# A decoder layer whose front end runs in segments of two, two and four token tiles instead of one, three and four

## The chip, the cores and the metric

One core of one Trainium2 chip runs the whole program; x holds 1024 tokens of 1024 features. The metric is the device time of one execution in microseconds; the kernel before has a median of 3162.57 us over 3 runs (3149.99 to 3165.83).

## What is computed

A decoder layer with adaLN modulation: shift, scale and gate vectors come from `silu(c) @ ada_w + ada_b`. The first half mixes tokens, with 8 retention heads and 8 stick-breaking attention heads behind one input projection and in front of one output projection. The second half is PEER, a layer of 16384 single-neuron experts of which each token picks 16 per head, 8 heads. Cut to what matters:

```python
h = rms_norm(x, norm1_gain) * (1 + scale1) + shift1
r_q, r_k, r_v, r_g, s_q, s_k, s_v = split(h @ w_in)            # 7 x 512 columns
y_ret = head_group_norm(retention(r_q, r_k, r_v)) * silu(r_g)
y_sb  = rms_norm(stick_breaking(rms_norm(s_q), rms_norm(s_k), s_v))
x = x + gate1 * (concat(y_ret, y_sb) @ w_out)
h2 = rms_norm(x, norm2_gain) * (1 + scale2) + shift2
# PEER, per token and head:
top_s, top_i = top_k(sub_scores(h2 @ w_query, sub_keys), 16)   # both halves of the query
best, ids = top_k(all sums of the two halves, 16)
act = gelu(h2 . down[ids]) * softmax(best)
x = x + gate2 * sum(act * up[ids])
```

## The kernel before, in words

The 1024 tokens are 8 token tiles of 128. The program has a front end, which goes through the tiles in segments, and two ways of computing PEER.

**The front end**, `seg_gen`, handles one segment of `nt` tiles from tile `t0`; `SEGS` (L25) lists the segments, (0,1), (1,3), (4,4). For its tiles a segment does, in this order: rms norm and transposition (`to_T`); seven streams of w_in (rk, rq, rv, rg, K, Q, V), each 8 weight blocks of 128x512 floats (256 KB); retention between the streams; stick-breaking attention, in units of a tile and a pair of heads; two streams of w_out; the residual, a second norm and transposition; four streams of wq, whose scores go to a top-16 on VectorE (`top16`), and the top-k over pairs (`topk`). That is 56, 16 and 32 weight blocks in each segment, whatever its number of tiles. The adaLN passes (`mod_pass`, L141) have 16, 16 and 8 loads of 512 KB in segment 0 and a smaller one in segment 1.

**`stream`** has two paths. With one tile (`whole`), weights come two blocks in one load of 512 KB into the pool `u`, 13 buffers (L256), and are multiplied as plain float32 (L261, L263). With more tiles the products are split float32r: each block is loaded into `wraw`, three buffers (L266); ScalarE copies it to the rounded `whi` (L71); POOL subtracts to get the rest, `wlo` (L271; VectorE for the first block of a stream, kt = 0); PE makes three products per tile, hi x hi, hi x lo, lo x hi (L275 to L281). The other operand is split likewise: `put` writes `Tlo` with a VectorE subtraction (L297).

**Tiles 0 to 3** use gathered expert rows (`gather_tile`): for each of the 128 picks of a token an indirect DMA issued by POOL brings a row of `down` for every token of the tile (L774, 512 KB), and VectorE takes the dot product (L785); then 128 times a row of `up` (L774) and an accumulation on VectorE (L795). That is 256 gathers a tile, 1024 in all, through four buffers `g`. The routing of tile 0 is made in four pieces of two heads (`topk(..., 2 * g, 2)`), each after its wq stream, so that gathers can start early; tiles 1 and 2 get theirs in one call for 8 heads; tile 3's scores go to DRAM and are routed late.

**Tiles 4 to 7** are computed densely against all experts (`dense`): first products from L826, second from L932, gate matrices built from one-hots (L865). Its first gate products follow the last piece of tile 4's routing.

**What sets the order.** A scheduler orders the instructions of each engine at build time, so any change of the program text moves rows everywhere. One tie is put in by hand: `HOLD = 480`; gathers 480 to 495 are issued only after the POOL operation of dense chunk 4, so no gather beyond 480 runs while the dense half builds its first gates.

The part that the change edits, at the end of the routing:

```python
        if t0 == 0:
            return []
        late = []
        for i in own[t0 == NG:]:
            f = lambda i=i: topk(kp, tv[i], ix[i], t0 + i, 0, 8)
            if t0 < NG:
                f()
            else:
                late.append(f)
```

`own` are the segment's tiles other than tile 3; `own[True:]` leaves out the first of them, which was routed in pieces.

Of the kernel before, what the change touches and what calls it, by code (L numbers as in the profile page):

```python
# [21 lines left out]
KT = D // 128  # L22
EPS = 1e-6
NT = 8
SEGS = [(0, 1), (1, 3), (4, 4)]  # L25
NG = 4
TD = (NT - NG) * 128
GB = 4
# [26 lines left out]
def tile_kernel(ctx, tc, A, out):  # L55
# [174 lines left out]
    def seg_gen(phase, t0, nt, hooks):  # L230
# [345 lines left out]
        for u in units:  # L576
            pend.append(u + (sb_weights(*u),))
            while after and len(pend) > 1:
                i = int(after.pop(0)[1])
# [49 lines left out]
        own = [i for i, t in enumerate(tiles) if t not in sc_d]  # L629
        tv = {i: kp.tile([128, 8, 2, 16], F32, name=f"tv{i}") for i in own}  # L630
        ix = {i: kp.tile([128, 8, 2, 16], U32, name=f"ix{i}") for i in own}
        for g in range(4):
# [18 lines left out]
            stream(A["wq"], 512 * g, hT[t0], ev_q, True)  # L651
            if t0 in (0, NG):
                topk(kp, tv[0][:, 2 * g:2 * g + 2], ix[0][:, 2 * g:2 * g + 2], t0, 2 * g, 2)
        if t0 == 0:
            return []
        late = []
        for i in own[t0 == NG:]:
            f = lambda i=i: topk(kp, tv[i], ix[i], t0 + i, 0, 8)
            if t0 < NG:
                f()  # L660
            else:
                late.append(f)
# [302 lines left out]
    with tc.tile_pool(name="tp", bufs=1) as tp_:  # L965
        kpg = tc.tile_pool(name="kp", bufs=1, side="right")
        kp = kpg.__enter__()
        with tc.tile_pool(name="att", bufs=1) as att:
            kTr = att.tile([128, 4, 1024], F32, name="kTr")
            vr = att.tile([128, NT, 512], F32, name="vr")  # L970
            state = att.tile([128, 4, 128], F32, name="state")
            POOL.memset(state, 0.0)
            with tc.tile_pool(name="wp", bufs=1) as wp, tc.tile_pool(name="up", bufs=13) as up, \
                    tc.tile_pool(name="vp", bufs=9) as vp:
                late = []
                for s in SEGS:
                    late = seg_gen((wp, tp_, up, vp, kp), *s, late)
        with tc.tile_pool(name="dp", bufs=1, reuse_waits="tile") as dp:
            hold = dense(*hT[NG], dp, kpg, late)
# [57 lines left out]
```

## Time and profile before

| | before |
|---|---|
| median of 3 runs | 3162.57 us (3149.99 to 3165.83) |
| the profiled execution's own time | 3159.11 us |
| its span | 3157.3 us |
| granted TensorE clock, mean | 0.914 |
| PE busy | 2680.1 us (85%) |
| VectorE (DVE) busy | 2539.2 us (80%) |
| POOL busy | 1938.5 us (61%) |
| ScalarE (ACT) busy | 1297.0 us (41%) |
| chain that ended last | DVE 24%, DMA 23%, PE 18%, issue 17%, POOL 14% |

Busy shares are means over the whole span. The kernel has stages with different limits, so the tables by stage (busy time of each engine in a stretch, in us from the span's start) say more than the page's totals; the timeline tells when the front end passes a given step. The stages of the profiled execution: segment 0 up to about 220 us, with the first gathers from 198 us; segment 1 from there to 766 us (first rotation at 259.51); segment 2 to 1505 us; then the dense half.

### The profile page before, as it was taken

What the parts mean: (1) busy time and instruction counts of PE and PEld (TensorE: products, weight loads), DVE (VectorE), ACT (ScalarE), POOL (GpSimd) and SP (SyncE); (2) the same over time, 40 slices, a digit from 0 to 9 for tenths busy, and PEclk for the clock granted to TensorE, in tenths of its full rate; (3) what the DMA queues carried; (4) which work ended last, traced back from release to release, by engine and by line L of the source; (5) the groups of instructions that cost most, each with busy time, mean ns of one, the idle gap of its engine ahead of it and who ended that gap; (6) DMA issues with size and microseconds to landing.
All of it is one profiled execution on the core that took longest, in us unless ns stands there. A gap on an engine that the chain in (4) does not pass through costs nothing.

```text
span 3157.3 us, 38775 instructions
## 1 busy us (share of the span) xinstructions
PE 2680.1 (85%) x12308; PEld 2078.8 (66%) x12308; DVE 2539.2 (80%) x4677; ACT 1297.0 (41%) x2254; POOL 1938.5 (61%) x1590
## 2 busy tenths in 40 slices
PE   6967878697886888762878999889999999999997
PEld 2454654486664446652767887677778878878886
DVE  2269788789988997899999778997767777777788
ACT  1232334344332652421666744454444434444441
POOL 1126775677777677652568756556666567666664
PEclk9978985899987879885999999999999999999998
DMA  8788877897867778882268889889989999999998
GB/s 320 252 295 285 285 250 248 298 341 254 268 228 243 226 238 281 299 279 95 111 238 328 313 304 328 282 303 318 332 308 332 323 332 334 332 328 332 321 337 273
DMA packets 337644, 899.20 MB, mean 285 GB/s; under 512 B 38296, under 2 KB 105880, under 8 KB 333344
## 3 DMA queue, kind: packets, MB, share of 16 engines
q0 software_dynamic: 147456, 536.94, 49.0%
q1 hardware_dynamic: 189984, 359.80, 32.9%
q8 instruction: 97, 1.59, 0.2%
q14 instruction: 107, 0.88, 0.1%
HBM read 846.24 MB, written 50.35 MB: 284 GB/s over the span
## 4 chain that ended last, share of the span: by engine, by line
DVE 24%; DMA 23%; PE 18%; issue 17%; POOL 14%; ACT 3%; SPq 1%; POOLq 0%; DVEq 0%; ACTq 0%
DMA g<-in_up_dram,ids 10%; POOL g L774 9%; DVE g L785 4%; DMA g<-in_down_dram,ids 4%; DVE gy L795 4%; DMA rawu<-in_up_dram 3%; PE acc L263 2%; DMA gm<-gd 2%; POOL u L817 2%; PE tp L826 2%; PE tp L827 2%; PE tp L828 2%; DVE dlo L817 1%; DVE p L865 1%; PE acc L932 1%
## 5 line engine op out<-in xcount | busy, mean ns | idle before, releaser
L774 POOL DMA_INDIRECT g<-in_down_dram,ids x512 | 582.5, 1138 | 461.9 <-DVE g L785 283.9
L795 DVE SCALAR_TENSOR_TENSOR gy<-g,a,gy 128x1024 f32<-128x1024 f32 x508 | 651.7, 1283 | 169.8 <-DMA g<-in_up_dram,ids 165.3
L774 POOL DMA_INDIRECT g<-in_up_dram,ids x512 | 552.2, 1078 | 364.5 <-DVE gy L795 197.4
L785 DVE SCALAR_TENSOR_TENSOR g<-g,gy 128x1024 f32<-128x1024 f32 x512 | 616.2, 1213 | 147.4 <-DMA g<-in_down_dram,ids 145.0
L826 PE MATMUL tp<-Thi,dhi 128*128 128x512 f32 x1024 | 405.2, 396 | 48.6 <-ACT dhi L71 45.3
L932 PE MATMUL acc<-u,p 128*128 128x512 f32 x1024 | 399.2, 399 | 42.9 <-ACT p L71 32.0
L828 PE MATMUL tp<-Thi,dlo 128*128 128x512 f32 x1024 | 402.8, 393 | 4.5 <-POOL dlo L817 4.0
L933 PE MATMUL acc<-u,p 128*128 128x512 f32 x1024 | 403.3, 397 | 0.0
L827 PE MATMUL tp<-Tlo,dhi 128*128 128x512 f32 x1024 | 403.1, 394 | 0.0
L934 PE MATMUL acc<-u,p 128*128 128x512 f32 x1024 | 385.1, 394 | 6.2 <-DVE p L911 6.1
L817 POOL TENSOR_TENSOR u<-rawu,u 128x1024 fp32r<-128x1024 f32 x128 | 308.9, 2415 | 53.1 <-ACT u L71 49.2
L271 POOL TENSOR_TENSOR wlo<-wraw,whi 128x512 fp32r<-128x512 f32 x182 | 236.0, 1304 | 61.6 <-ACT whi L71 33.9
L932 PEld LDWEIGHTS acc<-u,p 128*128 128x128 f32 x1024 | 196.3, 192 | 93.2 <-ACT p L71 37.9
L71 ACT ACTIVATE whi<-wraw 128x512 fp32r<-128x512 f32 x208 | 130.5, 630 | 308.5 <-DMA wraw<-in_w_in_dram 96.1
L817 DVE TENSOR_TENSOR dlo<-rawd,dhi 128x1024 fp32r<-128x1024 f32 x122 | 209.2, 1715 | 57.5 <-ACT dhi L71 54.6
L826 PEld LDWEIGHTS tp<-Thi,dhi 128*128 128x128 f32 x1024 | 194.4, 190 | 91.2 <-ACT dhi L71 46.3
L280 PE MATMUL acc<-wlo,Thi 128*128 128x512 f32 x504 | 213.2, 423 | 21.9 <-POOL wlo L271 19.5
L934 PEld LDWEIGHTS acc<-u,p 128*128 128x128 f32 x1024 | 194.6, 191 | 50.0 <-DVE p L911 9.6
L828 PEld LDWEIGHTS tp<-Thi,dlo 128*128 128x128 f32 x1024 | 194.4, 190 | 46.3 <-POOL dlo L817 5.1
L933 PEld LDWEIGHTS acc<-u,p 128*128 128x128 f32 x1024 | 196.5, 192 | 40.7
L827 PEld LDWEIGHTS tp<-Tlo,dhi 128*128 128x128 f32 x1024 | 194.6, 190 | 39.5
L71 ACT ACTIVATE u<-rawu 128x1024 fp32r<-128x1024 f32 x128 | 135.1, 1057 | 189.4 <-DMA rawu<-in_up_dram 182.1
(271 smaller groups left out, 5058.7 us busy)
## 6 DMA issues: line engine op xcount, KB each, us to landing
rawd<-in_downT_dram SPq DMA_DIRECT2D x128, 512.0 KB
rawu<-in_up_dram SPq DMA_DIRECT2D x128, 512.0 KB
gd<-u SPq DMA_DIRECT2D x32, 1024.0 KB
gm<-gd SPq DMA_DIRECT2D x512, 64.0 KB
wraw<-in_w_in_dram SPq DMA_DIRECT2D x112, 256.0 KB
u<-in_ada_w_dram SPq DMA_DIRECT2D x46, 512.0 KB
wraw<-in_wq_dram SPq DMA_DIRECT2D x64, 256.0 KB
u<-in_w_in_dram SPq DMA_DIRECT2D x28, 512.0 KB
```

What stands on the lines that cost most here:

```text
L71: ACT.activation(out_, in_, AF.Copy, scale=scale)
L271: (POOL if kt else DVE).tensor_sub(lo, raw, hi.bitcast(F32))
L774: POOL.indirect_dma_start(out=g, out_offset=None, in_=A[src], in_offset=bass.IndirectOffsetOnAxis(ap=groups[j // m][0][:, j % m:j % m + 1] ...
L785: DVE.scalar_tensor_tensor(g, g, 1.0, hp, op0=OP.mult, op1=OP.mult, accum_out=a[:, j:j + 1])
L795: DVE.scalar_tensor_tensor(y, g, a[:, j:j + 1], y, op0=OP.mult, op1=OP.add)
L817: eng.tensor_sub(lo, raw, hi.bitcast(F32))
L826: PE.matmul(a, dhi[:, sl], Hhi[:, kt], start=kt == 0, stop=False)
L827: PE.matmul(a, dhi[:, sl], Hlo[:, kt], start=False, stop=False)
L828: PE.matmul(a, dlo[:, sl], Hhi[:, kt], start=False, stop=kt == KT - 1)
L932: PE.matmul(y, phi[:, sl], uhi[:, ds_], start=st and b == 0, stop=False, skip_group_check=True)
L933: PE.matmul(y, phi[:, sl], ulo[:, ds_], start=False, stop=False, skip_group_check=True)
L934: PE.matmul(y, plo[:, sl], uhi[:, ds_], start=False, stop=sp and b == GB - 1, skip_group_check=True)
```

## The change

```diff
-SEGS = [(0, 1), (1, 3), (4, 4)]
+SEGS = [(0, 2), (2, 2), (4, 4)]
...
             if t0 in (0, NG):
                 topk(kp, tv[0][:, 2 * g:2 * g + 2], ix[0][:, 2 * g:2 * g + 2], t0, 2 * g, 2)
-        if t0 == 0:
-            return []
         late = []
-        for i in own[t0 == NG:]:
+        for i in own[t0 in (0, NG):]:
             f = lambda i=i: topk(kp, tv[i], ix[i], t0 + i, 0, 8)
```

Segment 0 now handles tiles 0 and 1, segment 1 tiles 2 and 3. No segment has one tile, so the `whole` path of `stream`, `operand`, `put` and `to_T` is not taken any more: segment 0 loads 104 weight blocks into `wraw` and splits each, and it splits its operands. Tile 0 is still routed in pieces; tile 1's 8-head routing follows in segment 0 instead of segment 1. Lines of the changed kernel from 656 on are two lower than those named here.

The order moves on every engine. Three places follow; rows that repeat are merged with a count.

SP's queue in segment 0, before, from the last w_in weights on (`ada` is the adaLN matrix, `L256` the large weight loads):

```order
L256 DMA u<-in_w_in_dram 128x2x512 x12
L482 DMA v<-in_decay_dram 128x512 x2
L483 DMA v<-in_xi_dram 128x512
L256 DMA u<-in_w_in_dram 128x2x512 x12
L138 DMA u<-in_ada_w_dram 128x1024 x15
L146 DMA v<-in_ada_b_dram 32x512 x4
```

The same place in the changed kernel:

```order
L266 DMA wraw<-in_w_in_dram 128x512 x33
L482 DMA v<-in_decay_dram 128x512 x2
L483 DMA v<-in_xi_dram 128x512
L266 DMA wraw<-in_w_in_dram 128x512 x20
L266 DMA wraw<-in_w_out_dram 128x512 x3
L138 DMA u<-in_ada_w_dram 128x1024 x12
L146 DMA v<-in_ada_b_dram 32x512 x2
L138 DMA u<-in_ada_w_dram 128x1024 x3
```

The 15 adaLN loads of the pass for gate1 and shift2 stand behind the w_in weights in both; but those weights now go through three buffers, each of which waits for the block before it, and three blocks of w_out stand between.

PE's order around that pass in the changed kernel (L141 are its products, L151 its transposes, L515 and L517 attention scores, L535 and L543 the transposes and values of attention):

```order
L515 MATMUL acc<-kTr,u 128x128
L517 MATMUL acc<-negm,ident 128x128
L141 MATMUL acc<-u,sc_159 32x512 x20
L151 MATMUL tp<-ident,v 128x128 x4
L535 MATMUL tp<-ident,u 128x128 x2
L543 MATMUL acc<-v,vr 64x128
```

Here the first attention transposes stand behind the pass's last products, as they do in the kernel before, with `x16` in place of `x20`.

POOL's queue at the first gathers, before (L80 and L81 are a norm's power of -1/2):

```order
L80 TENSOR_SCALAR s_918<-s_918 128x1
L81 TENSOR_TENSOR s_918<-s_918,mhalf 128x1
L774 DMA g<-in_down_dram,ids_0_1106 128x1024 x15
L80 TENSOR_SCALAR s_1580<-s_1580 128x1
L81 TENSOR_TENSOR s_1580<-s_1580,mhalf 128x1
```

And in the changed kernel (L772 is the gather's line there):

```order
L271 TENSOR_TENSOR wlo<-wraw,whi 128x512 x11
L80 TENSOR_SCALAR s_1989<-s_1989 128x1
L81 TENSOR_TENSOR s_1989<-s_1989,mhalf 128x1
L80 TENSOR_SCALAR s_1996<-s_1996 128x1
L81 TENSOR_TENSOR s_1996<-s_1996,mhalf 128x1
L271 TENSOR_TENSOR wlo<-wraw,whi 128x512 x17
L772 DMA g<-in_down_dram,ids_0_2355 128x1024 x4
L271 TENSOR_TENSOR wlo<-wraw,whi 128x512 x2
L772 DMA g<-in_down_dram,ids_0_2355 128x1024 x2
```

Two weight subtractions stand ahead of the first gather in the whole of POOL's queue before, 82 now, and behind it gathers and subtractions of wq alternate.

On VectorE the gathered rows that stand ahead of a step, before and after: first rotation of segment 1: 27 and 25; first rotation of segment 2: 220 and 185; end of segment 2's wq: 456 and 419; first one-hot of the dense half: 480 and 480. The 8-head top-k of tiles 1 and 2 ends behind 225 and 248 rows before, 48 and 184 now. VectorE has 39 weight subtractions for 26 and 64 `Tlo` subtractions for 46. At the end of the program the dense half's last output products stand behind 1018 to 1022 gathered rows before, and behind 1022 to 1024 now.

## Rows read from the trace of the kernel before

**Rows 1.** The page, part 1: busy time of each engine.
```profile
PE 2680.1 (85%) x12308; PEld 2078.8 (66%) x12308; DVE 2539.2 (80%) x4677; ACT 1297.0 (41%) x2254; POOL 1938.5 (61%) x1590
```

**Rows 2.** Table by stretch: length, busy PE, PEld, DVE, ACT, POOL, clock, DMA, GB/s.
```profile
0.00:199.00 199.00, 151.87 (x623) 74.31 (x624) 56.61 (x182) 42.69 (x93) 17.73 (x34) 0.93 0.82 293
...
257.00:766.00 509.00, 404.88 (x1807) 298.73 (x1808) 435.35 (x920) 185.74 (x337) 347.96 (x323) 0.84 0.83 282
257.00:1505.00 1248.00, 943.94 (x4358) 694.46 (x4359) 1099.45 (x2470) 452.26 (x809) 819.49 (x716) 0.84 0.76 256
1800.00:3157.00 1357.00, 1294.98 (x5600) 1059.74 (x5599) 1056.03 (x1456) 577.15 (x856) 851.08 (x630) 0.98 0.91 320
```

**Rows 3.** The same table for POOL's gather issues alone (L774; in brackets their number).
```profile
199.00:257.00 58.00, 27.17 (x28) 0.80 0.85 275
257.00:766.00 509.00, 198.66 (x191) 0.84 0.83 282
766.00:1505.00 739.00, 312.18 (x261) 0.83 0.72 238
```

**Rows 4.** Groups of VectorE instructions, 257 to 766 us: busy us, mean ns, idle before.
```profile
L785 DVE SCALAR_TENSOR_TENSOR g<-g,gy 128x1024 f32<-128x1024 f32 x103 | 124.1, 1212 | 28.3 <-DMA g<-in_down_dram,ids 28.0
L795 DVE SCALAR_TENSOR_TENSOR gy<-g,a,gy 128x1024 f32<-128x1024 f32 x88 | 112.8, 1282 | 18.9 <-DMA g<-in_up_dram,ids 18.3
...
L271 DVE TENSOR_TENSOR wlo<-wraw,whi 128x512 fp32r<-128x512 f32 x13 | 14.5, 1114 | 5.8 <-ACT whi L71 4.0 <-issue 1.5
...
L670 DVE MAX8 tv<-v 128x8 f32<-128x128 f32 x32 | 7.8, 281 | 1.2 <-ACT v L71 1.2
```

**Rows 5.** Waits (us, times, longest): VectorE's, 257 to 1505; SP's queue, 230 to 800.
```profile
DVE g L785 <- DMA g<-in_down_dram,ids: 56.3, 50, 4.5
...
SPq L266 <- POOL wlo L271: 329.3, 93, 34.8
```

**Rows 6.** Timeline (start, length) of segment 0 on PE, then markers on VectorE.
```profile
38.71 1.92 PE L263 MATMUL acc<-u,Thi 128*128 128x512 f32 x2
...
105.88 5.32 PE L263 MATMUL acc<-u,Thi 128*128 128x512 f32 x12
...
125.58 0.27 PE L535 MATMUL tp<-ident,u 128*128 128x128 f32 x1
...
136.58 5.38 PE L263 MATMUL acc<-u,Thi 128*128 128x512 f32 x8
...
145.03 8.85 PE L263 MATMUL acc<-u,Thi 128*128 128x512 f32 x20
...
202.72 1.22 DVE L785 SCALAR_TENSOR_TENSOR g<-g,gy 128x1024 f32<-128x1024 f32 x1 [1.41 <-DMA g<-in_down_dram,ids]
...
259.51 0.41 DVE L347 TENSOR_TENSOR v<-acc,cosT 128x256 f32<-128x256 f32 x1
...
1504.82 2.76 DVE L865 TENSOR_TENSOR p<-iota,rb 128x1024 bf16<-128x1024 bf16 x3
```

**Rows 7.** Timeline: loads issued by SP's queue, and one block's copy on ScalarE.
```profile
88.83 25.77 SPq L138 DMA_DIRECT2D u<-in_ada_w_dram  x15
...
243.79 9.53 SPq L266 DMA_DIRECT2D wraw<-in_w_in_dram  x5
...
433.43 0.33 SPq L266 DMA_DIRECT2D wraw<-in_w_in_dram  x1
...
436.26 0.63 ACT L71 ACTIVATE whi<-wraw 128x512 fp32r<-128x512 f32 x1 [2.32 <-DMA wraw<-in_w_in_dram]
```

**Rows 8.** Timeline, 243 to 248 us: a VectorE subtraction alone and beside POOL's.
```profile
243.85 0.55 DVE L297 TENSOR_TENSOR Tlo<-v,Thi 128x384 fp32r<-128x384 f32 x1
...
245.24 2.56 POOL L271 TENSOR_TENSOR wlo<-wraw,whi 128x512 fp32r<-128x512 f32 x2
245.46 2.76 DVE L297 TENSOR_TENSOR Tlo<-v,Thi 128x384 fp32r<-128x384 f32 x1
```

## Prediction

> **What bounds the kernel now.** The page first: TensorE (PE) is busy 85% of the span, VectorE (DVE) 80% [rows 1]. Those are averages over stages with different limits, so the table by stage comes next [rows 2]. From 1800 us to the end PE is busy 1295 of 1357 us: the dense half is bound by TensorE, and the change does not touch it. From 257 to 1505 us (segments 1 and 2 of the front end) the fullest engine is VectorE, 1099.45 of 1248 us or 88%; PE has 76%, POOL 66%. Before 199 us VectorE is busy 57 us of 199: the first segment leaves it idle, since no expert row can be gathered before a token tile is routed. The gathers fill the rest: 28, 191 and 261 are issued in the next three stretches [rows 3], 480 by 1505 us, where the hold stops them and the dense half's own work begins. A gathered row costs VectorE 1.21 us (dot product) or 1.28 us (accumulation) [rows 4].
>
> So the time until about 1505 us is the start of the gathers plus VectorE's remaining work at 88%. Of the idle 12% much is waiting for gathered rows (56 us for the "down" rows alone, rows 5), which will not vanish. The change puts more front-end work into the idle first segment, but makes that segment longer: it is weighed by these two terms.
>
> **Term 1: the first segment grows.** I follow segment 0 on PE [rows 6] and replace each piece.
>
> - *Seven w_in streams, 56 blocks of 128x512.* Now they run from 38.71 to 111.2 us, 72.5 us or 1.3 us per block, with plain float32 products and large loads far ahead into 13 buffers. After, each block goes through one of three raw buffers: load, ScalarE copy, POOL subtraction. One lightly loaded pass was 2.83 us from the issue to the copy's start (433.43 to 436.26), 0.63 us of copy [rows 7] and 1.28 us of subtraction (two in 2.56 us, rows 8), with hand-overs 4.95 us; over three buffers that is 1.65 us per block. Below, today's 1.3 us bounds it; above, the 2.3 us at which five loads were issued from 243.79 us on, (9.53 - 0.33)/4 [rows 7], with gathers between POOL's subtractions. Segment 0 has no gathers during its w_in streams, so I take 1.65, the light passes: 92.5 us, **+20** (0 to +56).
> - *A second tile's retention and attention, and the adaLN pass.* One tile's attention runs on PE from 125.58 to about 136.6 us, 11 us, with its first units hidden before. The second tile has twice the keys: 11 to 20, I take 16, and 3 for its retention between streams. The adaLN pass for gate1 and shift2 has 15 loads of 512 KB that today are issued from 88.83 us on, in 25.77 us [rows 7], 22 us ahead of the streams' end; in the new SP queue they stand behind the last V weight and three blocks of w_out, some 5 us ahead of the end at best. PE's order keeps the attention's transposes behind that pass, so 14 us (111.2 to 125.58) become 21 to 26: +8. Sum **+27** (+17 to +37).
> - *w_out, 16 blocks.* Today 17.3 us (136.58 to 153.88), loaded ahead. After, 16 x 1.65 = 26.4: **+9** (+4 to +20).
> - *Norms, transposes, routing.* One more tile to normalise and transpose here, one less in segment 1; wq's 32 blocks take 53 us by the same period, not far from now: **+4** (0 to +8).
>
> Together the first rotation of segment 1, now at 259.51 us, comes **+60** later (+35 to +105, as the ends do not all meet). The order has about as many gathers before it (25 for 27). The first gather itself, now consumed at 202.72 [rows 6], slips a few us more: in POOL's queue some 82 subtractions now stand ahead of it, 22 of them of wq.
>
> POOL's subtractions also bring something into this segment that it did not have: the same Tlo subtraction takes 0.55 us alone and 2.76 us beside two POOL subtractions [rows 8]. Between wq and the first index list some 15 to 20 two-input VectorE operations are on the path; their price is 0 to 20 us. I take 0: the chain mostly waits for wq's scores anyway, and most of its operations read one tensor. The Trainium skill, "SBUF — State Buffer", on the shared port pair, says that VectorE and GpSimd hold that pair exclusively for a whole instruction and the loser blocks; the 2.76 against 0.55 agrees, and it speaks against this change. By it I would add the 20 us here.
>
> **Term 2: VectorE has less to do afterwards.** From 257 to 766 us it was busy 435.35 us [rows 2]. Gathers were 124.1 + 112.8 = 237 of it, the kt = 0 weight subtractions 14.5 (they go by blocks, not tiles) [rows 4]. That leaves 184 for three tiles, of which two have their top-16 there (5 operations x 16 x 0.281 us = 22.5 us each, rows 4) and their top-k (no one row; 0 to 30 us each, I take 12). Front end of one tile: (184 - 45 - 24)/3 = 38 us. Tile 1's 38 us and its 22.5 of top-16 move into idle time of segment 0: 61 us. Its top-k stays behind that point (48 gathers stand before it in the order). With two gathers more still to do (+2.5): 1099.45 - 61 + 2.5 = 1041 us, which at 88.1% take 1182 us instead of 1248: **-66** (-45 to -80).
>
> **Term 3: the tail.** The dense half begins behind the same 480 gathers and keeps its order, so it shifts as a block; the last gathers come some four further ahead of the last output products: **-4** (0 to -5).
>
> At nothing I cost the 13 more weight subtractions and 18 more Tlo subtractions on VectorE: they fall into its idle time in segment 0, and without it would cost 13 x 1.1 + 18 x 0.55 = 24 us. ScalarE's 104 more copies are inside the block's period above.
>
> **Sum:** +60 - 66 - 4 = -10. On the profiled execution, 3159.1 us, that is 3149; on the median of the runs, 3162.6 (the profiled one is 3.5 below it), 3152.5. I say **3150**.
>
> **Rivals.**
>
> A, *VectorE alone counts* (faster). If blocks come at 1.4 us or so and the adaLN loads hide, segment 0 grows by 40; if the moved work is the upper 74 us, term 2 is -80. 40 - 80 - 4 = -44: 3118. For: VectorE is the fullest engine, 88%. Against: SP waited 329 us for POOL's subtractions between 230 and 800 us [rows 5], so the block chain is not free.
>
> B, *the block chain sets every segment's pace* (slower). Three raw buffers give a block 2.0 us or more whatever the number of tiles. Segment 0 then grows by 60 + 88 blocks in series x 0.35 = 90, while the streams of segment 1, with one tile less, do not get shorter; what shrinks there is attention and top-16, -60 at most. 90 - 60 - 4 = +26: 3188. It decides from some 1.8 us per block, where my sum is 88 x 0.15 = 13 us worse and back at zero. For: those 329 us. Against: the light passes of 4.95 us, and no gathers between the subtractions of segment 0.
>
> C, *the port* (no change). Each two-input VectorE operation between wq and the index list waits out one POOL subtraction of 1.28 us, 15 to 20 of them: +20, so +10 in all: 3170. For: rows 8. Against: few of these operations meet a subtraction while POOL also waits for blocks.
>
> **How the numbers follow.** A measurement of this kernel can tell about 0.5%, 16 us, from no change. Forecast 0.42 (its own range 3125 to 3172: faster by over 0.5% in 0.38 of it, within in 0.55, slower in 0.07), A 0.24 (faster), C 0.10 (0.8 of it within, the rest slower), B 0.24 (0.12 of it within, else slower). Faster 0.16 + 0.24 = 0.40; within 0.23 + 0.08 + 0.03 = 0.34; slower 0.26. The range reaches A's 3118 and B's 3188 with a little beyond each: 3112 to 3192.
>
> **What would show it.** Right: segment 0's w_in streams take about 92 us; the first gather is consumed near 270 us, the first rotation of segment 1 comes near 320, the dense half's first one-hot (L865, now at 1504.82, rows 6) near 1498, with VectorE at 85 to 91% between the last two. For A the streams take 80 us and that one-hot comes before 1465; for B they take over 110 us and the one-hot comes after 1520; for C the index list comes over 20 us after its last wq score. The forecast is wrong if VectorE's share leaves 85 to 91%, or if the time from the one-hot to the end moves by over 10 us.

## The result, and the profile after

The changed kernel takes 3269.38 us (median of 4 runs, 3260.02 to 3271.95) against 3160.41 us before: ratio 1.0337, 95% interval 1.0308 to 1.0367. It is 109 us slower; forecast were 3150 us, and the range ended at 3192. The profiled execution has a span of 3268.8 us, 111.5 more than before.

The page, part 1, of the changed kernel:

```profile
PE 2708.2 (83%) x12508; PEld 2109.9 (65%) x12508; DVE 2581.4 (79%) x4708; ACT 1359.3 (42%) x2373; POOL 2053.7 (63%) x1681
```

VectorE's share hardly moved, as averages do [rows 1]; POOL has 115 us more. The markers on the timeline, with start and length (lines from 656 on are two lower here, so L783 is the gather's dot product and L863 the one-hot):

```profile
45.29 0.78 PE L279 MATMUL acc<-whi,Thi 128*128 128x512 f32 x1
...
179.41 0.27 PE L535 MATMUL tp<-ident,u 128*128 128x128 f32 x1
...
231.64 0.75 DVE L562 SCALAR_TENSOR_TENSOR v<-v,cols,tp 128x512 f32<-128x512 f32 x1 [16.86 <-PE tp L561]
...
323.94 0.16 DVE L736 SCALAR_TENSOR_TENSOR ids<-ii 128x32 int32<-128x32 f32 x1
...
328.90 1.22 DVE L783 SCALAR_TENSOR_TENSOR g<-g,gy 128x1024 f32<-128x1024 f32 x1
...
392.93 0.40 DVE L347 TENSOR_TENSOR v<-acc,cosT 128x256 f32<-128x256 f32 x1
...
1603.39 2.74 DVE L863 TENSOR_TENSOR p<-iota,rb 128x1024 bf16<-128x1024 bf16 x3
```

Against [rows 6]: the first gathered row is consumed at 328.90 instead of 202.72 (+126), segment 1 begins to rotate at 392.93 instead of 259.51 (+133), and the dense half's first one-hot comes at 1603.39 instead of 1504.82 (+99). So segment 0 lost 133 us, segments 1 and 2 gave back 35, and another 13 were lost behind the one-hot. These markers come from one profiled execution of each kernel.

How VectorE stood in the two parts that the first gathered row divides. The table by stretch (length, then busy PE, PEld, DVE, ACT, POOL, clock, DMA share, GB/s), before:

```profile
0.00:202.70 202.70, 155.57 (x642) 78.01 (x643) 58.76 (x193) 43.14 (x95) 20.51 (x37) 0.92 0.82 293
202.70:1504.80 1302.10, 981.14 (x4568) 725.63 (x4567) 1150.73 (x2635) 476.40 (x862) 853.88 (x752) 0.83 0.77 257
```

and after:

```profile
0.00:328.90 328.90, 258.46 (x1240) 172.85 (x1240) 137.23 (x384) 131.77 (x261) 138.10 (x130) 0.91 0.53 175
328.90:1603.40 1274.50, 893.39 (x4167) 654.10 (x4168) 1123.24 (x2477) 449.14 (x816) 848.74 (x750) 0.81 0.79 264
```

Behind the first gathered row VectorE is busy 88.4% before and 88.1% after, and idle 151.4 us before and 151.3 after. Ahead of it, it is idle 143.9 us before and 191.7 after (+48). And its work up to the one-hot grew from 1209.5 to 1260.5 us (+51). 48 + 51 are the 99 us by which the one-hot is late. Half of the loss is thus idle time in segment 0, half is busy time that VectorE did not have before. This is a sum over one engine; it does not say that each saved microsecond would come back at the one-hot.

Segment 0 in pieces, on PE and by stretch, of the changed kernel:

```profile
45.00:113.00 68.00, 64.68 (x299) 49.77 (x299) 26.88 (x52) 34.56 (x62) 44.23 (x35) 0.98 0.53 148
113.00:160.00 47.00, 42.27 (x213) 30.74 (x212) 22.62 (x33) 20.79 (x37) 34.54 (x29) 1.00 0.51 158
179.00:194.00 15.00, 12.71 (x60) 7.45 (x60) 6.62 (x16) 8.44 (x29) 0.00 (x0) 1.00 0.00 1
194.00:200.00 6.00, 2.77 (x12) 2.69 (x13) 0.80 (x2) 0.97 (x3) 1.91 (x2) 0.50 0.00 0
200.00:218.00 18.00, 17.50 (x60) 9.62 (x58) 5.90 (x10) 7.53 (x20) 0.00 (x0) 0.50 0.74 258
```

The first row holds 40 weight blocks in 68 us, 1.7 us each. The second holds the other 16 in 47 us, 2.9 each: retention stands between them. PE is busy 65 of the 68 us and 42 of the 47, with six products a block, three for each tile. The last three rows are the attention. Tile 0's units run at a granted clock of 1.00 (2.4 GHz); at its closing norm (the one that ends a tile's attention) PE is busy 2.77 of 6 us, and from there to 218 us, with most of tile 1's units, the clock is 0.50 (1.2 GHz).

One stall of VectorE beside POOL's subtractions, in the timeline behind the first gathered row:

```profile
329.39 2.50 POOL L271 TENSOR_TENSOR wlo<-wraw,whi 128x512 fp32r<-128x512 f32 x2
...
330.05 1.90 DVE L705 TENSOR_SCALAR pq<-px 128x32 uint32<-128x32 uint32 x1
331.86 0.17 DVE L706 TENSOR_SCALAR pq<-px 128x32 uint32<-128x32 uint32 x1
```

A shift (L705) and a bitwise and (L706) of the same shape, each with one input tensor: beside the subtractions the shift takes 1.90 us, and the next operation, behind them, 0.17. The shortest shift of this shape in the trace took 0.16.

### The profile page after: what moved, and what is told of

It reads as the page before. It is cut to its first block, busy times and chain, and to the rows that moved or that the text cites. A ratio compares the mean times of both kernels' runs of the same rounds, so it can differ in the third digit from the quotient of the medians.

```text
span 3268.8 us, 39700 instructions
## 1 busy us (share of the span) xinstructions
PE 2708.2 (83%) x12508; PEld 2109.9 (65%) x12508; DVE 2581.4 (79%) x4708; ACT 1359.3 (42%) x2373; POOL 2053.7 (63%) x1681
## 5 line engine op out<-in xcount | busy, mean ns | idle before, releaser
L772 POOL DMA_INDIRECT g<-in_down_dram,ids x512 | 579.4, 1132 | 423.5 <-DVE g L783 282.4
L772 POOL DMA_INDIRECT g<-in_up_dram,ids x512 | 544.9, 1064 | 377.1 <-DVE gy L793 173.0
L783 DVE SCALAR_TENSOR_TENSOR g<-g,gy 128x1024 f32<-128x1024 f32 x512 | 615.5, 1213 | 159.2 <-DMA g<-in_down_dram,ids 156.6
L271 POOL TENSOR_TENSOR wlo<-wraw,whi 128x512 fp32r<-128x512 f32 x273 | 356.8, 1315 | 185.9 <-ACT whi L71 170.7
L71 ACT ACTIVATE whi<-wraw 128x512 fp32r<-128x512 f32 x312 | 194.8, 629 | 412.6 <-PE acc L281 125.2
L280 PE MATMUL acc<-wlo,Thi 128*128 128x512 f32 x576 | 248.1, 431 | 27.4 <-POOL wlo L271 24.4
L930 PEld LDWEIGHTS acc<-u,p 128*128 128x128 f32 x1024 | 197.0, 192 | 88.4 <-ACT p L71 39.0
L281 PE MATMUL acc<-whi,Tlo 128*128 128x512 f32 x576 | 236.7, 414 | 0.0
L279 PE MATMUL acc<-whi,Thi 128*128 128x512 f32 x576 | 203.2, 426 | 36.6 <-ACT whi L71 15.4
```

What stands on the lines that cost most here:

```text
L271: (POOL if kt else DVE).tensor_sub(lo, raw, hi.bitcast(F32))
L280: PE.matmul(acc[i], lhs_hi[:, kt, sl], lo, start=False, stop=False)
L772: POOL.indirect_dma_start(out=g, out_offset=None, in_=A[src], in_offset=bass.IndirectOffsetOnAxis(ap=groups[j // m][0][:, j % m:j % m + 1] ...
L783: DVE.scalar_tensor_tensor(g, g, 1.0, hp, op0=OP.mult, op1=OP.mult, accum_out=a[:, j:j + 1])
L930: PE.matmul(y, phi[:, sl], uhi[:, ds_], start=st and b == 0, stop=False, skip_group_check=True)
```

## The experiments

Twelve kernels; each was compared with the kernel before on the same chip. For all of them the markers are read as above: V stream's end, first gathered row, first one-hot.

**Split products alone.**

```diff
 # kernel before
-        whole = nt == 1
+        whole = False
```

> The segments of the kernel before (one, three and four tiles), but segment 0 with split products and the three-buffer weight path; nothing else changed. Theory T1 (the block chain is what made segment 0 126 us longer): 104 blocks at about 1.7 to 2.0 us in place of 1.3 us: first gathered row consumed 50 to 80 us later than the 202.7 us of the kernel before, median 3195 to 3240. Theory T2 (the second tile's serial retention, attention and norms made it longer, the weight path little): first gathered row at most 30 us later, median below 3185.

Measured: 3257.09 us, ratio 1.0304 [1.0241, 1.0368], +95 us.

```profile
0.00:262.50 262.50, 198.77 (x752) 122.86 (x752) 82.13 (x206) 99.87 (x199) 119.36 (x112) 0.78 0.62 207
262.50:1581.00 1318.50, 1017.55 (x4655) 759.11 (x4656) 1154.68 (x2653) 487.37 (x879) 867.12 (x768) 0.81 0.77 257
```

First gathered row at 262.5, 60 us later; one-hot at 1581, 76 later. Nothing was moved into segment 0, so nothing came back: VectorE still has 1154.7 us to do. The place is T1's, the median even above its interval. The split path alone (weights and operands, one tile) costs nearly what the whole change costs. Its seven streams take 107.5 us, against 75.7 before and 115.0 in the changed kernel:

```profile
39.60:106.40 66.80, 51.05 (x171) 32.76 (x171) 18.87 (x39) 31.57 (x57) 43.08 (x35) 0.82 0.57 158
106.40:147.10 40.70, 33.62 (x129) 16.06 (x128) 10.93 (x16) 16.14 (x31) 25.56 (x21) 0.87 0.75 264
```

The first row holds 40 blocks (1.7 us each), the second the other 16 (2.5 each), with one tile's retention. Part of this run's loss may be the clock: in the last 26 us before the first index list, in the wq streams, it was 0.50 here, with PE busy throughout, and 0.89 in the kernel before. The run does not separate the two.

```profile
232.00:258.00 26.00, 26.00 (x123) 25.82 (x122) 19.69 (x80) 12.24 (x27) 8.84 (x7) 0.50 0.29 95
```

The same part of the kernel before:

```profile
172.00:198.00 26.00, 19.20 (x154) 18.71 (x153) 14.31 (x79) 5.99 (x15) 0.00 (x0) 0.89 1.03 388
```

**Grouping alone.**

```diff
 # changed kernel
-        whole = nt == 1
+        whole = t0 == 0
```

> The changed segments (two, two, four), but segment 0 keeps plain float32 products and the large loads. PE then needs 14.9 us per w_in stream for two tiles (7.45 for one), 104 us for seven, near the 114 us measured with split products. T1: the rest of segment 0 (w_out, routing, adaLN pass) gets back what the block chain took: first gathered row near 265 us instead of 329, median below 3215. T2: first gathered row stays above 295 us, median 3230 to 3270.

Measured: 3273.7 us, 1.0352 [1.0297, 1.0407], +111 us; first gathered row at 334.1, one-hot at 1605.6. This is T2's side, the median 4 us above its interval. The groups of PE in its seven streams:

```profile
L263 PE MATMUL acc<-u,Thi 128*128 128x512 f32 x224 | 103.0, 616 | 0.0
```

and its table by stretch:

```profile
0.00:334.00 334.00, 284.81 (x1027) 153.54 (x1028) 98.86 (x340) 72.01 (x151) 31.57 (x50) 0.91 0.53 182
334.00:1605.60 1271.60, 908.60 (x4105) 659.83 (x4104) 1105.81 (x2483) 442.24 (x804) 828.88 (x739) 0.79 0.78 262
```

With plain products PE itself is nearly full, busy 131 of the streams' 142 us, 103 of them in products, where one tile needs half. VectorE's work to the one-hot is 1204.7 us, no more than before; the loss here is idle time in segment 0 (235 us of 334). So the two halves of the change do not add: with two tiles, the plain path is as slow as the split one. Neither theory holds alone.

**The subtractions of segment 0 on VectorE.**

```diff
 # changed kernel
-                (POOL if kt else DVE).tensor_sub(lo, raw, hi.bitcast(F32))
+                (POOL if kt and t0 else DVE).tensor_sub(lo, raw, hi.bitcast(F32))
```

> The changed kernel with all weight subtractions of segment 0 on VectorE (0.69 us each there) instead of POOL (1.29 us); VectorE is busy only 42% before the first gathered row. T1: the pass through a buffer gets 0.6 us shorter, 0.2 us per block over three buffers: first gathered row 15 to 25 us earlier than 329, median 3245 to 3255. T2: under 8 us earlier, median within 10 us of 3269. If the contention of POOL's subtractions with VectorE matters, the routing of tile 0 (from the last w_out product to the first index list, 64 us) shrinks by 10 us or more on top.

Measured: 3257.52 us, 12 less than the changed kernel. The V stream ends at 150.5 instead of 160.3 and attention at 216 instead of 232, but from w_out's end to the first index list it takes 80 us instead of 61: wq's subtractions now stand on VectorE ahead of the routing. First gathered row at 334.6, a miss for both theories; the one-hot comes 23 us earlier. Up to there VectorE is busy 20 us more than in the changed kernel, as it now does all the subtractions, and idle 43 less.

**Four raw buffers.**

```diff
 # changed kernel
-                raw = wp.tile([128, 512], F32, name="wraw", bufs=3)
+                raw = wp.tile([128, 512], F32, name="wraw", bufs=4)
```

> The changed kernel with four raw weight buffers instead of three, in all segments. T1: the period of a block falls from about 1.7 us toward PE's 1.35 us in segment 0, and where SP's queue waits for POOL's subtraction also in segments 1 and 2: first gathered row 20 to 35 us earlier than 329, median 3220 to 3245. T2: first gathered row at most 10 us earlier, median 3255 to 3270.

Measured: 3239.4 us, 30 less than the changed kernel: T1's median, but not T1's reason. The first gathered row comes at 321.6 (-7), the one-hot at 1594.1 (-9); another 15 us lie behind the one-hot, from where it took 1665 us to the last instruction in the changed kernel and 1650 here. Three buffers held segment 0 by a few us at most.

**The adaLN pass earlier.**

```diff
 # changed kernel; moved from behind the last w_in stream to behind the first
+        if t0 == 0:
+            mod_pass(2 * D, 4, lambda k: U([128, D]) if k else G(), V)
...
-        if t0 == 0:
-            mod_pass(2 * D, 4, lambda k: U([128, D]) if k else G(), V)
```

> The changed kernel with the adaLN pass for gate1 and shift2 written behind the first w_in stream instead of behind the last; nothing is left out. Theory T5 (late loads): the pass ended 18.6 us behind the last w_in stream, and the attention's transposes stand behind it; moved ahead, attention starts 12 to 18 us earlier and the first gathered row comes 10 to 18 us before 329; median 3250 to 3260. Rival T6: its 15 loads of 512 KB then stand between weight loads in SP's queue and lengthen the streams by as much: first gathered row within 6 us of 329, median within 8 us of 3269.

Measured: 3264.6 us; first gathered row at 331.3. The pass ends at 93 instead of 179 us, and the V stream ends 16 us later: T6. Moving the loads in SP's queue won nothing here. This run shows something else as well. Its table by stretch:

```profile
331.30:1605.20 1273.90, 905.41 (x4166) 659.86 (x4167) 1100.47 (x2477) 451.19 (x816) 843.58 (x750) 0.81 0.79 264
```

Behind the first gathered row VectorE is busy 23 us less than in the changed kernel (1123.2), and yet the one-hot comes 1274 us behind that row, as there. VectorE's busy time that goes away is not always time that is won.

**Attention units alternating.**

```diff
 # changed kernel
-        units = [(i, pr) for i in range(nt) for pr in range(4)]
+        units = [(i, pr) for pr in range(4) for i in range(nt)] if t0 == 0 else [(i, pr) for i in range(nt) for pr in range(4)]
```

> The changed kernel with the attention units of segment 0 in another order: the two tiles alternate instead of tile 0 first, so that both tiles' closing norms come at the end. Theory T7 (gap and clock): in the changed kernel PE stands idle about 6 us at tile 0's closing norm, and the granted clock is 0.50 from there on through tile 1's units (1.00 before); without the gap in the middle the clock stays at 1.00, the attention (53.5 us from the adaLN pass's end to the last closing norm) takes 36 to 42 us, first gathered row 12 to 18 us earlier, median 3250 to 3260. Rival T8 (tile 1's units are long by their own chain of ScalarE and VectorE work): attention at most 5 us shorter, median within 8 us of 3269.

Measured: 3272.97 us, no gain. In its table by stretch

```profile
178.00:194.00 16.00, 14.86 (x79) 9.05 (x79) 7.19 (x17) 8.90 (x30) 0.00 (x0) 1.00 0.00 1
194.00:224.00 30.00, 22.77 (x103) 15.88 (x103) 5.62 (x12) 11.44 (x29) 8.93 (x8) 0.83 0.59 202
```

the clock is 0.83 where it was near 0.5, attention takes 46 us instead of 53.5, and the first gathered row comes 9 us earlier, between T7 and T8. Then the gain is gone at the one-hot (1600.0, -3). The half clock was worth these 7 us of attention at most, as this edit changes the order of the units too.

**All three together**: four raw buffers, the earlier pass and the alternating units at once.

> The changed kernel with four raw weight buffers, the early adaLN pass and alternating attention units together. If the three are independent: the four buffers gave 30 us of median, the others 10 to 18 each by T5 and T7: median 3205 to 3225, first gathered row 290 to 300. By T6 and T8: 3235 to 3245. In neither case below the kernel before, since the split products alone cost 95 us there.

Measured: 3250.28 us, ratio 1.0291 [1.0234, 1.0348], no better than four buffers alone and above both forecasts; first gathered row at 342.1. They are not independent.

**The kernel before with four buffers and the early pass.**

> The kernel before (one, three and four tiles, plain products in segment 0) with four raw weight buffers and the early adaLN pass. If the block chain holds back segments 1 and 2 there too, as four buffers did in the changed kernel (30 us): median 3115 to 3145, first gathered row up to 10 us before 202.7. If VectorE alone sets the pace of segments 1 and 2: within 12 us of 3162.

Measured: 3154.07 us, 0.9975 [0.994, 1.001], no difference, as the second theory has it. First gathered row 12 us later, segment 1 from rotation to rotation 494 us instead of 511.

**A late start alone.** All work stays; the first 16 gathers are held until segment 1's first closing norm. The lines that hand that instruction over are left out below.

```diff
 # kernel before
+            r2 = rpow(r, r)
+            if t0 + i == 1:
+                first.append(r2.ins)
...
+            after_ = first[0] if n < 16 else hold if HOLD <= n < HOLD + 16 else None
+            with tc.issue_after(after_) if after_ is not None else nullcontext():
```

> The kernel before, with its first 16 gathers held until POOL has worked on the first closing norm of segment 1's attention (498 us in its trace; earlier here, as no gathers run beside it); nothing is left out and all work stays where it was. It asks what sets the time from the first gather to the dense half. Theory T9 (VectorE's remaining work at 88%): until then VectorE gets some 150 us of front-end work done, about 1000 us remain of 1151; with a first gathered row near 430 us the first one-hot of the dense half comes near 430 + 1000/0.884 = 1560 (1505 before), median 3205 to 3235. Theory T10 (a fixed pace of gathers: 480 of them took 1219 to 1266 us in ten kernels whatever VectorE had to do): 480 gathers end near 430 + 1245 = 1675, the one-hot at 1690 or later, median 3330 or more.

Measured: 3210.77 us, 1.0148 [1.011, 1.0186], +50 us. The first gathered row comes at 445.1, 242 us later, the one-hot at 1520.7, only 16 later. Its table by stretch, then the gather issues alone:

```profile
445.00:1521.00 1076.00, 749.53 (x3549) 561.54 (x3547) 958.32 (x2170) 375.45 (x666) 703.14 (x624) 0.80 0.80 267
```

```profile
445.00:1521.00 1076.00, 470.06 (x427) 0.80 0.80 267
```

T9's median and its rule: 958 us of work left, done at 89%. Its marker was 40 us off because only 426 gathered rows stand ahead of the one-hot instead of 480; the rest fell behind it. T10's marker and its median are out, by 170 and 119 us. Its pace is not: from the first row to the last one ahead of the one-hot a row took 2.53 us here, 2.60 before, and 2.54 to 2.64 in the other kernels. With less work for each row VectorE's share stayed, and the pace hardly moved; this run does not tell the two rules apart. So a start of the gathers that is later by 242 us costs less than half of what the change costs with 126 us. The reason is in the trace of before: no gather is issued there from 1450 to 1610 us, since all 480 that the hold allows are done. The gathers thus stood idle for 160 us; in this run, which has no such stretch, their late start used that up. The front end was not late: in this run segment 1 rotates first at 252.3 us, in the changed kernel at 392.9.

**Without tile 1's attention.**

```diff
 # changed kernel
+        units = [(i, pr) for i in range(nt) for pr in range(4) if t0 or not i]
+        if t0 == 0:
+            z0 = V((128, 4, 128))
+            POOL.memset(z0, 0.0)
+            put(mx, slice(4, 8), slice(128, 256), z0)
```

> The changed kernel without the stick-breaking attention of tile 1 (zeros take its place in w_out's operand), so with the second tile's attention off segment 0's path. T11 (all of it was on the path): first gathered row 30 to 40 us before 329, and the first one-hot of the dense half (1603) as much earlier: median 3230 to 3240. T12 (what is saved there is lost again behind it, as with the early adaLN pass and the alternating units): first gathered row under 20 us earlier, median within 15 us of 3269.

Measured: 3250.54 us. First gathered row at 300.2 (-29) and one-hot at 1575.9 (-28): just short of T11's 30 to 40. The last stretch takes 17 us more than in the changed kernel, and the median, 19 lower, lies between the two theories.

**Without the low part of segment 0's weights.** The products of wq lose theirs in the same way; those lines are left out below.

```diff
 # changed kernel
-                (POOL if kt else DVE).tensor_sub(lo, raw, hi.bitcast(F32))
+                if t0:
+                    (POOL if kt else DVE).tensor_sub(lo, raw, hi.bitcast(F32))
...
-                        PE.matmul(acc[i], lhs_hi[:, kt, sl], lo, start=False, stop=False)
+                        if t0:
+                            PE.matmul(acc[i], lhs_hi[:, kt, sl], lo, start=False, stop=False)
```

> The changed kernel without the low part of segment 0's weights: no subtraction on POOL or VectorE and no product hi x lo of the weights there (the operand's low part stays), so the link that ends each block's chain is gone: a pass through a raw buffer is 2.83 + 0.63 us, 1.2 us per block, PE 4 x 0.225 = 0.9. T1: the seven streams fall from 115 us to 85 or less, first gathered row 40 us or more before 329, median below 3235. Rival (retention and evacuations of two tiles set the last three streams, 2.9 us per block there against 1.7 in the first four): the streams stay above 95 us, first gathered row 15 to 35 us earlier, median 3235 to 3260.

Measured: 3216.29 us, 53 less than the changed kernel, the most that any single removal gave.

```profile
0.00:288.00 288.00, 227.53 (x1079) 145.97 (x1080) 111.94 (x402) 135.83 (x273) 29.95 (x48) 0.89 0.62 205
288.00:1552.00 1264.00, 882.66 (x4057) 640.90 (x4056) 1100.89 (x2444) 444.51 (x803) 837.05 (x741) 0.80 0.79 264
```

The streams fall from 115 to 92 us (45.4 to 137.6), above T1's 85; the first gathered row comes 41 us earlier and the one-hot 51. The edit takes away POOL's link and a third of PE's products at once, so it does not tell which of them set the pace. And VectorE's busy time up to the one-hot is 1212.8 us, 48 less than in the changed kernel, though only 13 subtractions of 0.7 to 1.3 us were VectorE's own. Most of the rest are stalls. I added up, from the trace, the VectorE instructions that took over twice the shortest of their kind and over 0.5 us more than it, by the POOL instruction beside them: with a weight subtraction beside them they lost 52 us up to the one-hot in the kernel before, 82 in the changed one, 52 in this one. With the subtractions of segment 0 on VectorE they lost 53, but with the adaLN pass earlier, where POOL has as many subtractions as in the changed kernel, only 57.

**The kernel before with four raw buffers.**

> The kernel before with four raw weight buffers and nothing else. With the early adaLN pass on top the first gathered row came 12 us later but segment 1 was 17 us shorter. If the early pass cost those 12 us and the buffers gave the rest: first gathered row within 3 us of 202.7, median 3140 to 3152. If four buffers are worth nothing where VectorE is full: within 8 us of 3161.

Measured: 3149.8 us, 0.9963 [0.9938, 0.9988], 11 us faster than before (12 runs against 17). First gathered row at 206.4, segment 1 at 503 us instead of 511: the median of the first theory, the first row just outside its 3 us. It is the fastest version of the study, 0.4% ahead of the kernel before.

## Why the prediction was wrong

**What bounds the kernel**: not refuted. From the first gathered row to the one-hot VectorE was busy 86 to 90% in all fourteen kernels, with 958 to 1155 us of busy time left. But the pace of the gathers was as steady, 2.53 to 2.64 us a row, and with the early adaLN pass 23 us less of busy time shortened nothing. That VectorE's work alone sets this stretch is not shown.

**Term 1 is the step that failed**: +60 to the first rotation, measured +133; to the first gathered row some 65, measured 126. By its parts, to the first gathered row:

- the start of the streams, not costed: 45.29 for 38.71, +7;
- the streams, +20: measured +39 (75.7 us to the last V transposition before, 115.0 after). The period of 1.65 came out for the first 40 blocks, 1.7, but its reason is not shown: PE is busy 95% of that time, a fourth raw buffer took 2 of the 69 us, and with half the products (split path, one tile) the pace was also 1.7. It was wrong to use it for the last 16, where retention stands between the blocks, 2.9 us each. The second tile is the smaller part of that: with one tile on the split path they took 2.5 each, with plain products 1.4. Which link sets that pace is open;
- the adaLN pass, +8: measured +8, though no order of loads could win it back;
- tile 1's attention, +16 and 3 for retention: measured +35 (18.2 us from the pass's end to the last closing norm before, 53.5 after). The 11 us that I took for one tile left out the part that today runs beside the adaLN pass and under w_out's products, and the clock was taken as constant;
- w_out, +9: measured +18 (from the last closing norm to w_out's end 11.9 us before, 30.0 after). In both kernels four of its blocks run ahead of that norm, here from 218.28 us; the other twelve took 2.3 us each after the change, adaLN products between them;
- norms and routing, +4: measured +19 (42.4 us from w_out's end to the first index list before, 61.5 after); some 6 of them are stalls of VectorE beside POOL's subtractions.

The pieces were priced by light rows of the trace of before, partly where other work stood beside them as cover. In segment 0 after the change less is covered: each block goes through SP, ScalarE and POOL to PE, which is itself busy 107 of the streams' 115 us. Each half of the change alone costs about as much as both (95 and 111 us), and no single removal gave back more than 53 of the 109.

**Term 2**, -66: measured -35 from the first rotation. The share held there, 88%; the work did not. Behind the rotation VectorE's busy time fell from 1097 to 1060 us, by 37 where I had 58.5. And up to the one-hot, segment 0 included, it grew by 51 us; I had costed its additions "at nothing". The additional subtractions themselves come to 15 us (24 costed). The larger part was stalls beside POOL's weight subtractions, 30 us more than before, of which 17 lie ahead of the first gathered row.

That is the mechanism of **rival C**, but not where C had it. Between w_out's end and the first index list the stalls came to some 6 us of its 20, so its argument against held there; the others are spread over the front end, which no term of mine covered. Most of them are two-input operations, as C has it (71 of the 82 us), but not all: the shift above reads one tensor and was held for 1.7 us all the same. The Trainium skill, "SBUF — State Buffer", in its section "SBUF: two separate sides", names two kinds of VectorE operation that take the pair of ports shared with GpSimd: those with two SBUF inputs, beside a GpSimd operation that reads SBUF, and those in a two-port mode. The 1.90 against 0.17 us fits the second kind, though no row shows an operation's mode; I had weighed only the first. What the stalls cost in the end is not shown: the seven kernels with 91 more subtractions on POOL than before, the changed one among them, have between 5 and 38 us more stalls, and the one with 5 more (the early adaLN pass) was hardly faster than the changed kernel.

**Term 3**, -4: measured +13. From the one-hot to the last instruction it took 1652 us before, 1665 in the changed kernel, and between 1639 and 1683 in the others but the late start (1696). The order there is nearly the same in all; what makes the difference was not found.

**The rivals.** A is out. B was nearest and right on the place: its signs came (streams of 115 us, the one-hot at 1603), but segment 0 grew by 133 where B had 90, and 3188 was 81 us too low. Its reason is not borne out: the pace of a block was not over 1.8 us in the first 40 blocks, four buffers gained 7 us up to the first gathered row, and segment 1 got 73 us shorter (438 for 511) where B allowed 60. The likeliest mistake of the reasoning as a whole was to treat VectorE's idle 144 us in segment 0 as room. It is time in which VectorE waits for the same chain that the change makes longer.

## What to carry to other kernels

An engine that idles in a stage is room for more work only if that work does not lengthen the chain which the engine waits for: price each moved piece by what that stage's chain does with no cover, its queues included, not by the lightest row of another stage. Ask of filler work (here the gathers) where it waits at its end, before its start is taken as critical: here 242 us of delay cost 50, where it had stood idle 160 us at a hold. And a GpSimd operation that is added can be paid on VectorE too: add up what VectorE's operations lose beside one that is there already, and do not take the sum for time that comes back.

## What was not expected of the hardware

- A VectorE shift of 128x32 integers with one input took 1.90 us beside a POOL subtraction and 0.16 at its shortest; a subtraction of 128x384 earlier showed 2.76 against 0.55 [rows 8].
- The granted clock of PE fell from 1.00 to 0.50 in a stretch of 6 us of which PE was busy 2.77, and stayed there for the next 18 us, although PE was busy 17.5 of them. With another order of units, at 0.83, attention was 7 us shorter, and nothing was left of it at the end.
